# Layer 0 of a hybrid decoder trunk: the second value group and the second gate group multiplied as one pair, with seven products for eight on half of the rows

## The chip, the core and the metric

The kernel runs on one core of one Trainium2 chip. The core has TensorE (PE, matrix multiply; its weight loads are shown as PEld), VectorE (DVE), ScalarE (ACT), GpSimd (POOL) and SyncE (SP). Here POOL and SP do little else than start transfers from HBM. Each engine works through its own queue in a fixed order; engines wait for each other through semaphores. The metric is the device time of one execution in microseconds (us); the program is built once with a fixed order on every engine.

## What is computed

The input is 256 tokens of 2048 numbers in float32. Layer 0 norms them and multiplies by one wide weight, `w_in` (2048 x 6144). Its columns feed an RG-LRU (x and y, eight blocks of 128 columns each) and eight HGRN2 heads (query q and forget gate f, 128 columns a head, a value v and an output gate g):

```python
proj = h @ w_in
x_lru, y_lru, q_h, f_h, v_h, g_h = jnp.split(proj, list(IN_SPLITS), axis=-1)
lru = rg_lru(causal_depthwise_conv(x_lru, conv_w, conv_b), w_a, b_a, w_i, b_i, lam)
lru = lru * jax.nn.gelu(y_lru.astype(F32), approximate=True)
hg = hgrn2(q_h, f_h, v_h, g_h, lower_bound, g_norm)
mixed = jnp.concatenate([lru, hg], axis=-1).astype(h.dtype)
return mixed @ w_out
```

An output projection with residual, a squared-ReLU MLP, an attention layer (layer 1) and a second MLP follow. The change concerns v and g of heads 4 to 7 only: 512 columns of v and 512 of g, each of them 256 tokens x 2048 rows of weight.

## The kernel before

**Arithmetic.** Every float32 factor is split into a high part (rounded to the fast matmul format, fp32r) and a low remainder. A product takes three matmuls: high x high, high x low, low x high. For a weight tile, class `Weights` does the split: a copy on ACT makes `hi` (line 109), a subtraction on DVE makes `lo` (line 110). A *unit* is one weight tile of 128 partitions x 2048 columns (1 MB). It goes through pools of three buffers each: `raw` from HBM, `hi`, `lo`.

**Plan of units.** `units` lists all weight tiles in the order of use. `fetch()` starts a unit's load on SP's queue and issues its split, some three units ahead of use, with raised priority (`stream`). `unit()` hands the split tile to its user. The mixer of layer 0 is written as a string of steps (`ORDER`): `v0`, `v1` value groups and `k0`, `k1` gate groups (four units each), `h0` to `h7` heads (two units each), `x0` to `x7` and `y0` to `y7` LRU blocks (one unit each), `g0`, `g1` LRU gates (one unit each). A scheduler then fixes each engine's order by priorities: work that is not urgent is put where an engine would be free by its estimate. The matmuls `mm` stay in the written order.

**Value and gate groups.** `tokens()` multiplies a group: two PSUM banks (one for each half of the 256 tokens), four units, each unit with 4 blocks of 128 rows. That is 2 x 16 x 3 = 96 matmuls with 512 columns. The transposed, scaled input lies in `bufa` as 16 blocks of 128 rows, high and low. ACT takes the result out of PSUM with the factor `rt`, one over the root mean square of each token; the gate group then gets `v * sigmoid(v)` (lines 428 to 430).

**The first norm.** `rt` comes from `xtok`, the input by tokens, which lies in `xall` (its view by tokens is called `xres`) and stays there as the residual until the output projection adds to it (line 598). ACT squares it (line 272), DVE forms the mean and its inverse square root in 13 small steps (lines 276 to 305), PE turns the result over tokens (line 288). Because this is needed soon, the second half of the low part of units 6 and 7 (the third and fourth unit of `k0`) must come after the last step of the root on DVE:

```python
behind[6] = behind[7] = [roots[-1]]
```

**Seven products.** The later layers already multiply with `blocks()`. It takes two column groups of weights together, and on the first 8 of 16 row blocks it forms seven products for eight: the four quarters of the input (two halves of tokens, even and odd row blocks) and the four quarters of the weights are combined by sums beforehand, in the manner of Strassen and Winograd. The sums over the input are called *forms* (in the output projection lines 634 and 584 to 587, then a cast, 580, and a subtraction, 581). The sums over the weights are made on DVE (lines 141 and 161) and by accumulating loads on POOL's queue (lines 153 and 163), in two arrays `t1` and `s` of 1 MB each. The order of a pair is a, t1, t2, n, c, n, t3, d, n, t4, n: seven products and four plain units of the other 8 row blocks (each with two products). One product is 4 blocks x 3 = 12 matmuls of 512 columns.

**Heads.** After q and f, a head runs a chain: a multiplication on DVE (line 484) and a small matmul on PE (line 467) alternate seven times, then come line 462 and lines 491 to 493. The chains are spread between the large matmuls of later steps.

Of the kernel before, what the change touches and what calls it, by code (L numbers as in the profile page):

```python
# [20 lines left out]
P = 128  # L21
S = 256
# [20 lines left out]
def trunk_kernel(ctx, tc, begin, xtok, cols, tab, masks, pos, fin, w_in, w_gate, w_out, w_qkv, w_o, w1, w2, out):  # L43
# [31 lines left out]
    def order(src, i):  # L75
        return LASTS if src is w2 and i == 120 else ORDERS
# [21 lines left out]
    class Weights:  # L98
# [17 lines left out]
        def part(self, at, n):  # L116
            return self.hi[:, at:at + n], self.lo[:, at:at + n]
# [17 lines left out]
    def combine(u, src, i, what, i0):  # L135
        def load(name, j, home=wraw):
            held[name] = home.tile([P, 2048], F32, name="raw" if home is wraw else name)
            nc.sync.dma_start(held[name], src[j])

        def add(to, x, y):  # L140
            V.tensor_tensor(held[to], held[x], held[y], OP.add)
# [12 lines left out]
        if ahead == ("t4",) and src is w2 and i0 != BOUNDARY:  # L154
            add("s", "s", "d")
        w = made[u] = Weights(held[{"t1": "s", "t2": "s", "t3": "t1", "t4": "s"}.get(what, what)],
                              1024 if what == "t2" else 2048, follow=what == "t2" or u and units[u - 1][2:3] == ("t2",))
        if what == "t1":
            for at in (0, 1024):
                s = held["s"][:, at:at + 1024]  # L160
                V.tensor_tensor(s, s, held["c"][:, at:at + 1024], OP.add)  # L161
        if what == "c" and (src is not w2 or i0 == BOUNDARY):
            nc.gpsimd.dma_start(held["s"], src[i0 + 1], accum_op=OP.add)
# [28 lines left out]
    def mm(*args, **kw):  # L192
        chain[:] = [after(T.matmul(*args, **kw), chain)]  # L193
# [7 lines left out]
    def put_off(wait, *fs):  # L201
        later.extend((clock[0] + wait, f) for f in fs)
# [215 lines left out]
    def hgrn_v(i):  # L418
# [3 lines left out]
                A.activation(v[:, j], v[:, j], AF.Copy, scale=rt[:, j:j + 1])  # L422
        return v

    def hgrn_g(i):
        v = tokens_group(w_in, 16 + i * 16, rt, name="gg")
        for j in range(2):
            z = wk.tile([P, 512], F32, name="gs", bufs=1)
            lut(z, v[:, j], AF.Sigmoid)
            V.tensor_tensor(v[:, j], v[:, j], z, OP.mult)  # L430
        return v

    def hgrn(hd, vg, gg):
# [112 lines left out]
    def lru_out(b):  # L546
# [8 lines left out]
        V.tensor_tensor(y, y, xc[:, b], OP.mult)  # L555
        split_to(bufb[:, b], y)

    vgroups, ggroups = {}, {}
    for step in ORDER.split():
        i = int(step[1])  # L560
        if step[0] == "v":
# [16 lines left out]
    def part_forms(f, k, m, at, src):  # L578
        hi, lo = (f[:, k:k + m, h].rearrange("p m (f c) -> p m f c", f=4)[:, :, at] for h in range(2))
        A.copy(hi, src)  # L580
        V.tensor_tensor(lo, src, hi.bitcast(F32), OP.subtract)

    def combos(s1, s2, s3, s4, a11, a21, a12, a22):
        V.tensor_tensor(s1, a21, a22, OP.subtract)
        V.tensor_tensor(s3, a11, a21, OP.subtract)
        V.tensor_tensor(s2, s1, a11, OP.subtract)
        V.tensor_tensor(s4, a12, s2, OP.add)
# [40 lines left out]
    def out_project(src, gname, off):  # L628
        nrm = Norm()

        def forms(k):
            z = pair.tile([P, 2, 2, P], F32, name="y21", bufs=2)
            h, l = (bufb[:, k + off:k + off + 2, c * S:c * S + S].bitcast(F32) for c in range(2))
            V.tensor_tensor(z.rearrange("p i j c -> p i (j c)"), h, l, OP.add)
            a11, a21, a12, a22 = (z[:, i, j] for i in range(2) for j in range(2))
            combos(a22, a11, a21, a12, a11, a21, a12, a22)
            part_forms(formh, k // 2, 1, slice(0, 4), z.rearrange("p i j (one c) -> p one (i j) c", one=1))

        put_off(4, *(lambda k=k: forms(k) for k in range(0, 8, 2)))
# [6 lines left out]
    cosT = cst.tile([P, 2, 16], F32, name="cosT")  # L646
    sinT = cst.tile([P, 2, 2, 16], F32, name="sinT")


    def blocks(src, i0, n0, mov, forms, events, final, off=0):  # L650
        part = lambda k, c: mov[:, (k + off) % KB, c * P:c * P + P]
        plain = lambda j, k: (part(k, j), part(k, 2 + j))
        form = lambda f, k: (forms[:, k, 0, f * P:f * P + P], forms[:, k, 1, f * P:f * P + P])
        side = {"a": lambda i: plain(0, 2 * i), "d": lambda i: plain(0, 2 * i + 1), "t4": lambda i: plain(1, 2 * i + 1),
                "t1": lambda i: form(3, i), "t2": lambda i: form(0, i), "t3": lambda i: form(1, i),
                "c": lambda i: form(2, i)}
        alpha, delta, gamma = (pmm.tile([P, 512], F32, name="p") for _ in range(3))
        beta = psc.tile([P, 512], F32, name="pt" if src is w_qkv else "po" if n0 else "pd", bufs=1)
        bank = {"a": beta, "t1": alpha, "t2": beta, "c": alpha, "t3": beta, "d": gamma, "t4": beta}
        sums = {(0, 0): gamma, (0, 1): beta, (1, 0): alpha, (1, 1): delta}  # L660
        opened = [gamma, delta]
        starts = {"a": (gamma, beta), "t1": (delta, alpha)}

        def times(bank, w, get):
            for i in range(4):
                h, l = w.part(i * 512, 512)
                xh, xl = get(i)
                mm(bank, xh, h, start=not any(b is bank for b in opened), stop=False, skip_group_check=True)
                opened.append(bank)
                mm(bank, xh, l, start=False, stop=False, skip_group_check=True)  # L670
                mm(bank, xl, h, start=False, stop=i == 3, skip_group_check=True)

        plains, twice = [0, 0, 0, 0], {}
        for what, u, *js in order(src, i0 + 4 * n0):
            if js != [(1,)]:
                w = unit(src, None if u is None else i0 + 4 * n0 + u)
                twice[u] = w
            else:
                w = twice[u]
            if what != "n":  # L680
                times(bank[what], w, side[what])
                if what in starts:
                    with urgent():
                        A.copy(*starts[what])
                if what in events:
                    events[what](bank[what])
                flush(1, 1)
                continue
            n, g = divmod(u, 4)
            for j in js[0] if js else (1, 0) if n or src is w_qkv else (0, 1):  # L690
                times(sums[n, j], w, lambda i, j=j, g=g: plain(j, 4 * g + i))
                plains[2 * n + j] += 1
                if plains[2 * n + j] == 2:
                    final(n, j, sums[n, j])
                flush(1, 1)

    def to_h(n, tiles):
        def work():
# [370 lines left out]
def _layout(a):  # L1069
# [14 lines left out]
    wi = n(a["rec_w_in"][0])  # L1084
    fx = feat(wi[:, :2048])
    fq = feat(wi[:, 2048:4096])
    fg = toks(wi[:, 5120:])
    fv = toks(wi[:, 4096:5120])
    w_in = [fx]
    for g in range(2):  # L1090
        if g:
# [50 lines left out]
```

## Time and profile before

| | |
|---|---|
| median of 3 runs | 2135.94 us (2135.84 to 2135.94) |
| the profiled execution | 2135.02 us |
| its span, first to last instruction | 2133.1 us |
| PE busy | 2122.7 us |
| DVE busy | 1776.4 us |
| ACT busy | 1372.5 us |
| POOL busy | 65.0 us |
| mean granted clock of TensorE | 0.999 |

The profile is of one execution. Times inside it count from the span's start. The page gives the busy time of each engine; the chain goes back from the last instruction through what released each step; the timeline lists instructions in order (start, duration, engine, line, operation; out<-in with shapes; xN means N merged instructions; in brackets the engine's idle time ahead of it and what ended it); the table of windows gives each engine's busy time in a stretch. Matmuls overlap, so the duration of one is longer than its distance to the next. An fp32 matmul that is not split (the small ones of the heads) shows as two records. A few per cent of the matmul records can be missing.

### The profile page before, as it was taken

The page shows a single profiled execution, that of the slowest core. Times are in us where ns is not written, and L with a number is a line of the kernel's source. Part 1 is how long each engine was busy: PE and PEld are TensorE (multiplying, and loading weights), DVE is VectorE, ACT ScalarE, POOL GpSimd, SP SyncE. Part 2 cuts the span into 40 slices and gives each one's busy share as a digit, 9 for nine tenths or more (in the row PEclk, how much of TensorE's full clock was granted, in tenths as well). Part 3 has the DMA queues.
Part 4 walks back from the last instruction along what each step waited for, and adds up shares of the span by engine and source line. Part 5 has one row for each costly group of instructions (what it writes and reads, how often), then busy time and mean ns, then how long its engine had stood idle before and what let it go on. Part 6 is the DMA issues. An engine that isn't in the chain of part 4 may idle for free.

```text
span 2133.1 us, 26744 instructions
## 1 busy us (share of the span) xinstructions
PE 2122.7 (100%) x10554; PEld 1799.9 (84%) x10554; DVE 1776.4 (83%) x1961; ACT 1372.5 (64%) x1545; POOL 65.0 (3%) x83
## 2 busy tenths in 40 slices
PE   9999999999999999999999999999999999999998
PEld 8989998888888888888888888888888888888886
DVE  7767888888888888888987777698887888888887
ACT  7445565766576567567667767666756765755764
POOL 0000000000000000000000000000000000000000
PEclk9999999999999999999999999999999999999999
DMA  8444446686777677777887667667767768777873
GB/s 340 158 173 157 160 145 217 212 271 227 236 239 254 221 238 253 236 242 232 265 272 224 230 208 250 233 217 226 248 234 252 238 209 266 243 234 226 272 225 145
DMA packets 69518, 486.62 MB, mean 228 GB/s; under 512 B 7776, under 2 KB 8288, under 8 KB 11920
## 3 DMA queue, kind: packets, MB, share of 16 engines
q1 hardware_dynamic: 58176, 410.96, 51.2%
q0 software_dynamic: 10928, 73.60, 17.8%
q8 instruction: 83, 1.36, 0.3%
q10 hardware_dynamic: 288, 0.34, 0.0%
q14 instruction: 43, 0.35, 0.0%
HBM read 480.68 MB, written 4.19 MB: 227 GB/s over the span
## 4 chain that ended last, share of the span: by engine, by line
PE 98%; ACT 1%; DVE 1%; DMA 0%; issue 0%; ACTq 0%; DVEq 0%
PE p L193 62%; PE po L193 14%; PE pd L193 12%; PE pt L193 5%; PE pl L196 2%; PE pl L467 1%; PE pl L193 0%; ACT hi L109 0%; DMA raw<-in_w 0%; DVE lo L110 0%; PE po L252 0%; PE pd L196 0%; PE pd L451 0%; PE pl L462 0%; PE po L492 0%
## 5 line engine op out<-in xcount | busy, mean ns | idle before, releaser
L110 DVE TENSOR_TENSOR lo<-raw,hi 128x2048 fp32r<-128x2048 f32 (+2 forms) x406 | 790.1, 1955 | 174.6 <-ACT hi L109 169.8
L109 ACT CAST hi<-raw 128x2048 fp32r<-128x2048 f32 (+2 forms) x406 | 660.1, 1643 | 338.4 <-PE p L193 178.8
L193 PE MATMUL p<-hi,bufa 128*128 128x512 f32 x1488 | 481.6, 394 | 0.0
L193 PE MATMUL p<-hi,bufb 128*128 128x512 f32 x1264 | 406.6, 391 | 0.0
L193 PEld LDWEIGHTS p<-hi,bufa 128*128 128x128 f32 x1488 | 279.4, 188 | 56.6
L110 DVE TENSOR_TENSOR lo<-s,hi 128x2048 fp32r<-128x2048 f32 (+1 forms) x160 | 279.0, 1754 | 27.4 <-ACT hi L109 26.3
L109 ACT CAST hi<-s 128x2048 fp32r<-128x2048 f32 (+1 forms) x160 | 236.7, 1480 | 98.9 <-DVE s L161 54.7
L193 PE MATMUL p<-lo,bufa 128*128 128x512 f32 x744 | 287.5, 390 | 0.0
L193 PEld LDWEIGHTS p<-hi,bufb 128*128 128x128 f32 x1264 | 237.2, 188 | 48.9
L193 PE MATMUL p<-lo,bufb 128*128 128x512 f32 x632 | 246.0, 389 | 0.0
L193 PE MATMUL p<-bufa,hi 128*128 128x256 f32 x1024 | 193.2, 287 | 0.0
L193 PEld LDWEIGHTS p<-lo,bufa 128*128 128x128 f32 x744 | 139.9, 188 | 27.4
L193 PEld LDWEIGHTS p<-bufa,hi 128*128 128x128 f32 x1024 | 161.2, 191 | 0.2
L193 PE MATMUL p<-bufa,lo 128*128 128x256 f32 x512 | 146.5, 286 | 0.0
L109 ACT CAST hi<-t 128x2048 fp32r<-128x2048 f32 x40 | 76.6, 1914 | 99.9 <-PE p L193 91.4
L110 DVE TENSOR_TENSOR lo<-t,hi 128x2048 fp32r<-128x2048 f32 x40 | 91.7, 2292 | 57.7 <-ACT hi L109 57.3
L193 PEld LDWEIGHTS p<-lo,bufb 128*128 128x128 f32 x632 | 118.7, 188 | 24.0
L193 PE MATMUL p<-hi,formx 128*128 128x512 f32 x352 | 115.8, 390 | 0.0
L193 PE MATMUL po<-hi,bufb 128*128 128x512 f32 x320 | 103.5, 390 | 0.0
L193 PEld LDWEIGHTS p<-bufa,lo 128*128 128x128 f32 x512 | 98.1, 192 | 0.0
L193 PE MATMUL p<-hi,formh 128*128 128x512 f32 x288 | 94.5, 389 | 0.0
L161 DVE TENSOR_TENSOR s<-s,raw 128x1024 f32<-128x1024 f32 x80 | 94.0, 1216 | 0.0
(301 smaller groups left out, 3208.2 us busy)
## 6 DMA issues: line engine op xcount, KB each, us to landing
raw<-in_w SPq DMA_DIRECT2D x224, 1024.0 KB, 6.0
raw<-in_w_in SPq DMA_DIRECT2D x44, 1024.0 KB, 4.8
raw<-in_w_qkv SPq DMA_DIRECT2D x42, 1024.0 KB, 6.9
t<-in_w SPq DMA_DIRECT2D x32, 1024.0 KB, 4.9
t<-in_w POOLq DMA_DIRECT2D x32, 1024.0 KB, 8.6
s<-in_w POOLq DMA_DIRECT2D x17, 1024.0 KB, 8.5
raw<-in_w_out SPq DMA_DIRECT2D x15, 1024.0 KB, 4.9
raw<-in_w_o SPq DMA_DIRECT2D x15, 1024.0 KB, 4.9
```

What stands on the lines that cost most here:

```text
L109: a = A.copy(h, w)
L110: v = V.tensor_tensor(l, w, h.bitcast(F32), OP.subtract)
L161: V.tensor_tensor(s, s, held["c"][:, at:at + 1024], OP.add)
L193: chain[:] = [after(T.matmul(*args, **kw), chain)]
L196: chain[:] = [after(T.transpose(out_, in_, ident), chain)]
L467: T.matmul(pl[:, j], kq[:, js], halves(qp[:, js], c, True), start=True, stop=True)
```

## The change

`v1` and `k1` become one step `p1`, which runs `blocks()` on `w_in` from unit 28 on. Four new steps `f0` to `f3` make the forms of the input's first 8 row blocks. The forms lie in parts of `bufb` that are still free then (blocks 12 to 15 and 4 to 7). The weight sums `t1` and `s` use the two halves of `xall`, which after the first norm holds only the residual; after the pair, `xtok` is loaded a second time through POOL's queue. `blocks()` gets a case for `w_in`: three PSUM banks at first, and the fourth when it comes to `d`; some partial results are taken out of PSUM by ACT and completed by additions on DVE (`put`, `add`). The weights of the second groups are laid out in the order of `PAIRED`. The step string also has x3, h3 and x0 behind the pair instead of ahead of the groups, some other LRU blocks in another order, and y7 ahead of y3. `part_forms`, `combos` and `blocks` are moved up in the file; `forms` of the output projection becomes `pair_forms`.

```diff
     for step in ORDER.split():
+        if step[0] == "p":
+            plan2(w_in, 28)
+        if step[0] not in where:
+            continue
...
         if what == "a":
-            load("t1", i0 + 4, both)
+            if src is w_in:
+                held["t1"], held["s"] = xall[:, :2048], xall[:, 2048:]
+                nc.sync.dma_start(held["t1"], src[i0 + 4])
+            else:
+                load("t1", i0 + 4, both)
+                held["s"] = both.tile([P, 2048], F32, name="s")
             load("a", i)
-            held["s"] = both.tile([P, 2048], F32, name="s")
             add("s", "a", "t1")
...
         alpha, delta, gamma = (pmm.tile([P, 512], F32, name="p") for _ in range(3))
-        beta = psc.tile([P, 512], F32, name="pt" if src is w_qkv else "po" if n0 else "pd", bufs=1)
+        if src is w_in:
+            beta, gamma = gamma, None
+        else:
+            beta = psc.tile([P, 512], F32, name="pt" if src is w_qkv else "po" if n0 else "pd", bufs=1)
...
-        opened = [gamma, delta]
-        starts = {"a": (gamma, beta), "t1": (delta, alpha)}
+        opened, starts = [], {}
+        if src is not w_in:
+            opened, starts = [gamma, delta], {"a": (gamma, beta), "t1": (delta, alpha)}
...
+            if what == "d" and bank["d"] is None:
+                bank["d"] = sums[0, 0] = pmm.tile([P, 512], F32, name="p")
...
+    def pair_forms(forms, k, src, z):
+        h, l = (src[:, k:k + 2, c * S:c * S + S].bitcast(F32) for c in range(2))
+        V.tensor_tensor(z.rearrange("p i j c -> p i (j c)"), h, l, OP.add)
+        a11, a21, a12, a22 = (z[:, i, j] for i in range(2) for j in range(2))
+        combos(a22, a11, a21, a12, a11, a21, a12, a22)
+        part_forms(forms, k % 8 // 2, 1, slice(0, 4), z.rearrange("p i j (one c) -> p one (i j) c", one=1))
...
+    def values_gates():
+        both_ = [vgs.tile([P, 2, 512], F32, name=n) for n in ("vg", "gg")]
+        rn = tmp.tile([P, 2], F32, name="rn0", bufs=1)
+        V.tensor_scalar(rn, rt, -1.0, None, op0=OP.mult)
+
+        def put(n, j, r=rt):
+            def event(bank):
+                with urgent():
+                    A.activation(both_[n][:, j], bank, AF.Copy, scale=r[:, j:j + 1])
+            return event
+
+        def add(n, j, bank, r=rt):
+            o = both_[n][:, j]
+            with urgent():
+                V.scalar_tensor_tensor(o, bank, r[:, j:j + 1], o, op0=OP.mult, op1=OP.add)
+
+        def final(n, j, bank):
+            if (n, j) == (0, 1):
+                put(n, j)(bank)
+            else:
+                add(n, j, bank)
+            if (n, j) == (1, 0):
+                gated(both_[1], 0)
+
+        def u3(bank):
+            add(1, 1, bank, rn)
+            gated(both_[1], 1)
+
+        blocks(w_in, 28, 0, bufa, form0,
+               {"a": put(0, 0), "t1": put(1, 1), "t2": put(1, 0, rn), "t3": u3}, final)
+        for j in range(2):
+            nc.gpsimd.dma_start(xres[:, j], xtok[:, j])
+        return both_
...
+        if step[0] == "f":
+            pair_forms(form0, 2 * i, bufa, wk.tile([P, 2, 2, P], F32, name="fz", bufs=1))
+        elif step[0] == "p":
+            vgroups[1], ggroups[1] = values_gates()
...
-ORDER = "v0 k0 h0 h1 h2 x1 x3 h3 x0 k1 v1 x2 h4 x4 g0 x5 h5 h6 x6 y0 y1 h7 x7 g1 y3 y7 y4 y2 y5 y6"
+ORDER = "v0 k0 h0 f0 f1 h1 f2 f3 x1 h2 p1 h3 x3 x2 h4 x0 x5 g0 x4 h5 h6 x6 y0 y1 h7 x7 g1 y7 y3 y4 y2 y5 y6"
```

More of the change, by code (lines that the diff above doesn't have):

```diff
@@ L423, in hgrn_v, with gated @@
         return v
+    def gated(v, j):
+        z = wk.tile([P, 512], F32, name="gs", bufs=1)
+        lut(z, v[:, j], AF.Sigmoid)
+        V.tensor_tensor(v[:, j], v[:, j], z, OP.mult)
     def hgrn_g(i):
@@ L556, in lru_out, with part_forms, combos @@
         split_to(bufb[:, b], y)
+    def part_forms(f, k, m, at, src):
+        hi, lo = (f[:, k:k + m, h].rearrange("p m (f c) -> p m f c", f=4)[:, :, at] for h in range(2))
+        A.copy(hi, src)
+        V.tensor_tensor(lo, src, hi.bitcast(F32), OP.subtract)
+    def combos(s1, s2, s3, s4, a11, a21, a12, a22):
+        V.tensor_tensor(s1, a21, a22, OP.subtract)
+        V.tensor_tensor(s3, a11, a21, OP.subtract)
+        V.tensor_tensor(s2, s1, a11, OP.subtract)
+        V.tensor_tensor(s4, a12, s2, OP.add)
@@ new lines, in blocks, with times @@
+    def blocks(src, i0, n0, mov, forms, events, final, off=0):
+        part = lambda k, c: mov[:, (k + off) % KB, c * P:c * P + P]
+        plain = lambda j, k: (part(k, j), part(k, 2 + j))
+        form = lambda f, k: (forms[:, k, 0, f * P:f * P + P], forms[:, k, 1, f * P:f * P + P])
+        side = {"a": lambda i: plain(0, 2 * i), "d": lambda i: plain(0, 2 * i + 1), "t4": lambda i: plain(1, 2 * i + 1),
+                "t1": lambda i: form(3, i), "t2": lambda i: form(0, i), "t3": lambda i: form(1, i),
+                "c": lambda i: form(2, i)}
+        alpha, delta, gamma = (pmm.tile([P, 512], F32, name="p") for _ in range(3))
+        if src is w_in:
+            beta, gamma = gamma, None
+        else:
+            beta = psc.tile([P, 512], F32, name="pt" if src is w_qkv else "po" if n0 else "pd", bufs=1)
+        bank = {"a": beta, "t1": alpha, "t2": beta, "c": alpha, "t3": beta, "d": gamma, "t4": beta}
+        sums = {(0, 0): gamma, (0, 1): beta, (1, 0): alpha, (1, 1): delta}
+        opened, starts = [], {}
+        if src is not w_in:
+            opened, starts = [gamma, delta], {"a": (gamma, beta), "t1": (delta, alpha)}
+        def times(bank, w, get):
+            for i in range(4):
+                h, l = w.part(i * 512, 512)
+                xh, xl = get(i)
+                mm(bank, xh, h, start=not any(b is bank for b in opened), stop=False, skip_group_check=True)
+                opened.append(bank)
+                mm(bank, xh, l, start=False, stop=False, skip_group_check=True)
+                mm(bank, xl, h, start=False, stop=i == 3, skip_group_check=True)
+        plains, twice = [0, 0, 0, 0], {}
+        for what, u, *js in order(src, i0 + 4 * n0):
+            if js != [(1,)]:
+                w = unit(src, None if u is None else i0 + 4 * n0 + u)
+                twice[u] = w
+            else:
+                w = twice[u]
+            if what == "d" and bank["d"] is None:
+                bank["d"] = sums[0, 0] = pmm.tile([P, 512], F32, name="p")
+            if what != "n":
+                times(bank[what], w, side[what])
+                if what in starts:
+                    with urgent():
+                        A.copy(*starts[what])
+                if what in events:
+                    events[what](bank[what])
+                flush(1, 1)
+                continue
+            n, g = divmod(u, 4)
+            for j in js[0] if js else (1, 0) if n or src is w_qkv else (0, 1):
+                times(sums[n, j], w, lambda i, j=j, g=g: plain(j, 4 * g + i))
+                plains[2 * n + j] += 1
+                if plains[2 * n + j] == 2:
+                    final(n, j, sums[n, j])
+                flush(1, 1)
@@ new lines, in pair_forms, with __getitem__ @@
+    def pair_forms(forms, k, src, z):
[4 more added lines that the diff above has]
+        part_forms(forms, k % 8 // 2, 1, slice(0, 4), z.rearrange("p i j (one c) -> p one (i j) c", one=1))
+    class Apart:
+        def __getitem__(self, at):
+            k = at[1]
+            i = k.start if isinstance(k, slice) else k
+            b = bufb[:, (12, 4)[i // 2]:][:, :4].rearrange("p (k h) c -> p k h c", h=2)
+            return b[(at[0], slice(i % 2, i % 2 + 1) if isinstance(k, slice) else i % 2) + at[2:]]
@@ new lines, in trunk_kernel @@
+    form0 = Apart()
+    def values_gates():
[9 more added lines that the diff above has]
+            o = both_[n][:, j]
+            with urgent():
+                V.scalar_tensor_tensor(o, bank, r[:, j:j + 1], o, op0=OP.mult, op1=OP.add)
+        def final(n, j, bank):
+            if (n, j) == (0, 1):
+                put(n, j)(bank)
+            else:
+                add(n, j, bank)
[9 more added lines that the diff above has]
+        return both_
@@ L576, in open_pairs @@
         return pool_, pool_.tile([P, 4, 2, 512], F32R, name="formh")
[L578 to L587, printed above, removed]
     both = ctx.enter_context(tc.tile_pool(name="both", bufs=1))
@@ L629, in out_project @@
         nrm = Norm()
[L631 to L639, printed above, removed]
+        put_off(4, *(lambda k=k: pair_forms(formh, k + off, bufb, pair.tile([P, 2, 2, P], F32, name="y21", bufs=2))
+                     for k in range(0, 8, 2)))
         for n in range(2):
@@ L647, in trunk_kernel @@
     sinT = cst.tile([P, 2, 2, 16], F32, name="sinT")
[L650 to L657, printed above, removed]
-        beta = psc.tile([P, 512], F32, name="pt" if src is w_qkv else "po" if n0 else "pd", bufs=1)
-        bank = {"a": beta, "t1": alpha, "t2": beta, "c": alpha, "t3": beta, "d": gamma, "t4": beta}
-        sums = {(0, 0): gamma, (0, 1): beta, (1, 0): alpha, (1, 1): delta}
-        opened = [gamma, delta]
-        starts = {"a": (gamma, beta), "t1": (delta, alpha)}
[L664 to L695, printed above, removed]
@@ L1086, in _layout @@
     fq = feat(wi[:, 2048:4096])
-    fg = toks(wi[:, 5120:])
-    fv = toks(wi[:, 4096:5120])
+    fg, fv = (np.concatenate([toks(w[:, :512]), toks(w[:, 512:], PAIRED)]) for w in (wi[:, 5120:], wi[:, 4096:5120]))
     w_in = [fx]
```

6 lines of the change are left out of this document (2 added, 4 removed).

## The prediction, made before the changed kernel had run

> **What bounds the kernel now.** I read the page first, then the table of windows over the first layer's mixer, then the chain of work that ended last.
>
> ```profile
> PE 2122.7 (100%) x10554; PEld 1799.9 (84%) x10554; DVE 1776.4 (83%) x1961; ACT 1372.5 (64%) x1545; POOL 65.0 (3%) x83
> PE 98%; ACT 1%; DVE 1%; DMA 0%; issue 0%; ACTq 0%; DVEq 0%
> ...
> core 0: us, PE busy (x) PEld busy (x) DVE busy (x) ACT busy (x) POOL busy (x), PEclk, DMA share, GB/s
> 0.00:40.00 40.00, 38.95 (x172) 33.17 (x173) 31.57 (x106) 32.46 (x64) 0.89 (x5) 1.00 0.88 348
> 40.00:80.00 40.00, 40.00 (x297) 38.18 (x297) 26.15 (x43) 19.86 (x26) 0.00 (x0) 1.00 0.62 213
> 120.00:160.00 40.00, 40.00 (x204) 33.88 (x203) 25.48 (x55) 18.09 (x28) 0.00 (x0) 1.00 0.51 177
> 200.00:240.00 40.00, 40.00 (x341) 40.00 (x341) 35.45 (x95) 28.76 (x59) 0.00 (x0) 1.00 0.46 156
> 280.00:320.00 40.00, 39.73 (x328) 38.96 (x327) 35.24 (x89) 30.62 (x63) 0.00 (x0) 1.00 0.42 146
> ```
>
> TensorE is the bound: 98% of the chain is PE, and in the mixer it stands still for 1.05 us at the start and 0.27 us near 285 us. So a matmul taken away is worth its full time, and any wait put before a matmul costs its full time. There is hardly a stall that the change could remove. The margin lies in VectorE: 25 us of 40 where the second groups stand now (120:160), 35 of 40 after them.
>
> **Matmuls.** The two groups are 2 x 2 x 16 x 3 = 192 matmuls of 512 columns. Afterwards 7 x 4 x 3 = 84 do the first eight rows of blocks and 96 the rest: 180. The order of the changed program's matmul queue has 12 fewer and is otherwise made of the same shapes. The chain has one product of twelve by itself:
>
> ```profile
> 6.55 34.36 PE p L193 x151
> 415.77 2.72 PE pd L193 x12
> ```
>
> Term one: -2.72 us, all on the path.
>
> **Forms (f0 to f3), new.** Four times a sum over 512 columns, four combinations of 128, a cast on ACT and a subtraction over 512. The same lines run today in the output projection:
>
> ```profile
> 342.91 1.29 DVE L581 TENSOR_TENSOR formh<-y,formh 128x512 fp32r<-128x512 f32 x2
> 344.11 1.29 DVE L634 TENSOR_TENSOR y<-bufb 128x512 f32<-128x512 f32 x2
> 345.31 0.49 DVE L584 TENSOR_TENSOR y<-y 128x128 f32<-128x128 f32 x2
> 345.71 0.29 DVE L585 TENSOR_TENSOR y<-y 128x128 f32<-128x128 f32 x1
> L580 ACT CAST formh<-y x40: 606/620/632, 341.4 to 2023.8; 128x512 fp32r<-128x512 f32 x40
> ```
>
> Two of 512 start 1.20 us before what follows, two of 128 0.40 us: a form is 0.6 + 4 x 0.2 + 0.6 = 2.0 us of VectorE, the four 8.0, and 4 x 0.62 = 2.5 us of ACT. In the order of the changed program they do not lie after h0 where the step string puts them, but as filling in the opening and in the first gate group. There they meet this:
>
> ```profile
> 23.51 3.08 DVE L110 TENSOR_TENSOR lo<-raw,hi 128x512 fp32r<-128x512 f32 x3
> 27.82 0.62 PE L193 MATMUL p<-lo,bufa 128*128 128x512 f32 x2
> 31.28 0.17 DVE L871 TENSOR_SCALAR sinT<-ang 128x32 f32<-128x32 f32 x1
> 33.51 0.62 ACT L272 ACTIVATE z<-xall 128x512 bf16<-128x512 f32 x1
> 34.26 0.16 DVE L276 TENSOR_REDUCE nm<-ss 128x2 f32<-128x8 f32 x1 [2.80 <-ACT z L272]
> 35.56 1.22 DVE L110 TENSOR_TENSOR lo<-raw,hi 128x1024 fp32r<-128x1024 f32 x1
> 37.68 0.16 DVE L305 SCALAR_TENSOR_TENSOR nr<-rs,nr 128x2 f32<-128x2 f32 x1
> 37.76 3.49 DVE L110 TENSOR_TENSOR lo<-raw,hi 128x1024 fp32r<-128x1024 f32 x3
> 40.74 0.38 PE L288 MATMUL pt<-tab__199,nr 128*128 128x128 f32 x2
> 40.88 0.48 PE L193 MATMUL p<-lo,bufa 128*128 128x512 f32 x1
> ```
>
> These rows are the root of the first norm: ACT squares (L272), 13 small VectorE steps from L276 to L305, then the second half of the third gate unit's low part (its first half is the row at 35.56), which `behind` orders after the root. At 40.74 PE turns the root and at 40.88 needs that second half. It begins at 37.76, takes 1.14 and is ready 2.0 us early. I add up what the changed order puts ahead of it:
> - Start of the root. VectorE was free at 31.45 and waited 2.80 us for ACT. Ahead of L276 now stand all of f0 and f1 and f2 short of its last combination and its subtraction: 2.0 + 2.0 + 1.2 = 5.2 us, of which some 0.6 falls into small gaps of the opening. VectorE arrives at 31.45 + 4.6 = 36.0. ACT, with one cast among the squares and the first group ending 0.3 late (f0 makes the third and fifth low blocks of the opening just too late), would have been ready at 35.2. So the root starts at 36.0, 1.8 late.
> - Length of the root. It was 37.76 - 34.26 = 3.50 us. Now the last combination of f2 (0.2), its subtraction (0.6), the sum of f3 (0.6), three of its combinations (0.6) and the first half of the fourth unit's low part (1.14) lie in it, 3.1 us, of which 0.6 fills latency between dependent steps: about 6.0 us.
> - So the second half begins at 42.0 and is ready at 43.2, against 40.9 needed. Term two: +2.3 us, on the path. Behind that wait on PE stands everything. Next late would be the fourth unit's halves, which follow at 1.14 each and are needed 5 us later: covered.
>
> Bounds of term two: 0 if the order's filling falls into idle time on the chip as well (2.80 us were idle), 4.0 if none of it does (5.2 + 3.1 against the margins of 2.8 and 2.0, and 0.5 for the opening). I take 2.3, nearer to the upper end, because the filling is in the queue ahead of the waiting rows and not beside them.
>
> **The pair itself.** Eleven units are prepared instead of eight, and weights are added up.
>
> ```profile
> 350.42 0.69 DVE L598 SCALAR_TENSOR_TENSOR xall<-p,xall 128x512 f32<-128x512 f32 x1 [0.39 <-PE p L193]
> 353.97 2.28 DVE L141 TENSOR_TENSOR s<-raw,t 128x2048 f32<-128x2048 f32 x1
> 364.14 2.29 DVE L110 TENSOR_TENSOR lo<-raw,hi 128x2048 fp32r<-128x2048 f32 x1 [1.32 <-ACT hi L109]
> L161 DVE TENSOR_TENSOR s<-s,raw 128x1024 f32<-128x1024 f32 x80 | 94.0, 1216 | 0.0
> raw<-in_w_in SPq DMA_DIRECT2D x44, 1024.0 KB, 4.8
> s<-in_w POOLq DMA_DIRECT2D x17, 1024.0 KB, 8.5
> ```
>
> VectorE: 3 more low parts x 2.2, one sum 2.2, two half sums x 1.14, four additions from PSUM x 0.6 = 13.5 us more. ACT: three more casts of about 1.9 = 5.7 us; its four copies from PSUM stay four. Between the first product and the next head, 43 us of PE, the changed VectorE queue holds 36 us including the tails of h0 to h2, so it is covered. Walking the queue with these rows, each low part of the pair is ready 1 to 5 us before its product; the tightest is the first whole unit, 0.9 us. The sum of the first two units waits in VectorE's queue for two loads; the later of them can start when x1's low part is made, 10 us before the sum; h2's low part behind it has 5 us. On SP's queue the load into the residual's array needs no slot, so nothing stands behind it. On POOL two accumulating loads, 8.5 us each, come 30 and 10 us before their use; the two reloads of the residual stand behind them and before the next accumulate, some 200 us before the residual is read. DMA has room: share 0.51 in 120:160, and two accumulates and two reloads are new. Price: 0.
>
> **The order of steps.** x3, h3 and x0 move from before the groups to behind them. From the end of the pair to the eighth y the queues hold 113 us of VectorE beside 132 of PE. On average covered, but around the first gates the margins between a chain's multiplication and its matmul shrink from this
>
> ```profile
> 221.12 0.42 DVE L484 TENSOR_TENSOR qk<-qk,tot 128x256 f32<-128x256 f32 x1
> 222.60 0.55 PE L467 MATMUL pl<-qk 128*128 128x64 f32 x4
> ```
>
> (1.1 us) to 0.3 to 0.5 us by the same walk, at four places. Bounds: 0 if the walk is right, about 1 us at each of the four if VectorE is 1.4 us later. I take +0.5, nearer zero, as a late chain lets the next work slide in. y3 and y7 trade places at no cost: same shapes, same queues from h6 on.
>
> **Sum.** -2.72 + 2.3 + 0.5 = +0.1. The profiled execution took 2135.02, its span 2133.1; the median of the runs is 2135.94, 0.9 above it. I apply the sum to the median: 2136.0 us. 0.2% is 4.3 us, about what a measurement can tell from no change.
>
> **Rivals.**
> - The saving arrives whole: the forms run in VectorE's idle time before the root. For it: the 2.80 us idle above. Against it: their place ahead of the low half. 2135.9 - 2.7 = 2133.2. To pass -4.3 us another 1.6 would have to come from stalls of which the mixer shows 0.3.
> - Slower: the dense stretch after the pair. At 35 of 40 us VectorE has 5 us in 40; were each operation there waiting 0.15 us more on ACT or PE, the 180 rows between pair and h6 would lose 27 us against 19 of slack, so it decides once VectorE falls 19 us behind: then PE waits 27 - 19 = 8 us, less the 2.7 saved: 2141.
> - TensorE's clock falls in the wait at the root. Cold and warm price of one shape:
>
> ```profile
> 1.05 5.49 PE po L252 x24
> 67.10 0.45 PE pd L451 x4
> ```
>
> 229 ns against 112. If a wait of 2.3 to 4 us starts another such 5.5 us, half of it is lost: 2136.0 + 2.7 = 2138.7. Against it: the clock is 1.00 in every window. The Trainium skill, "TensorE: Matmul & The Clock Gate", section "Part 1: The HAM clock gate", says that an idle window of about 3.4 us brings the clock back to half, and as much activity releases it; by that rule a wait of 2.3 us would mostly escape and one of 4 us would not. No row of this trace has an idle time to test it.
>
> **How the numbers follow.** Forecast 0.63; saving whole 0.17; dense stretch 0.13; clock 0.07. All but the dense case and part of the clock case lie within 0.2%: faster 0.04, same 0.79, slower 0.17. The range goes from the whole saving with the mixer's small stalls (2132.6) to the dense case (2141.5). Within the forecast's own case: 2134 to 2138.
>
> **What the profile after would show.** 12 matmuls of 512 columns fewer. PE waiting 2 to 3 us near 41 us for L114 or the root. No PE wait inside the pair. VectorE near 36 of 40 us from 130 to 170. PE's end of the mixer within 1 us of today's. I am wrong if PE shows no wait near 41 us, or waits of several us after the pair.

## The result and the profile after

The changed kernel takes 2165.14 us, median of four runs (2164.73 to 2165.76), against 2135.94 us: 1.0139 times as long, 95% interval 1.0127 to 1.0150. That is 29.2 us slower, and 23.6 us beyond the upper end of the predicted range.

The page of the changed kernel, its busy times and its chain, and then the table of windows over the first layer's mixer (columns as in the prediction):

```profile
PE 2151.1 (99%) x10542; PEld 1797.9 (83%) x10542; DVE 1798.5 (83%) x1989; ACT 1380.8 (64%) x1545; POOL 67.6 (3%) x87
PE 97%; DVE 1%; ACT 0%; DMA 0%; issue 0%; SPq 0%; ACTq 0%; DVEq 0%
...
0.00:40.00 40.00, 38.25 (x165) 31.60 (x166) 33.56 (x116) 31.69 (x65) 0.89 (x5) 1.00 0.95 372
40.00:80.00 40.00, 38.21 (x271) 35.57 (x270) 30.17 (x51) 21.80 (x28) 0.86 (x1) 1.00 0.55 192
120.00:160.00 40.00, 40.00 (x251) 35.94 (x250) 31.02 (x60) 19.70 (x27) 0.55 (x1) 1.00 0.65 234
200.00:240.00 40.00, 40.00 (x341) 40.00 (x340) 35.70 (x93) 28.98 (x58) 0.00 (x0) 1.00 0.43 146
280.00:320.00 40.00, 39.71 (x328) 38.93 (x328) 35.02 (x91) 29.61 (x62) 0.00 (x0) 1.00 0.43 151
```

From here on a *product* is one matmul of 512 columns. TensorE has 12 products fewer and is busy 28.4 us longer. In the first 80 us it is idle for 2.5 us more than before; from there on no wait of it is longer than 0.4 us. The loss is busy time. To see where, the same three places are looked up in the timelines of TensorE: the last products ahead of the root's transposition, the first matmul of 256 columns behind the first gate group, and the first product behind the mixer. Before:

```profile
40.29 0.61 PE L193 MATMUL p<-hi,bufa 128*128 128x512 f32 x2
...
50.27 0.40 PE L193 MATMUL p<-bufa,hi 128*128 128x256 f32 x2
...
328.17 0.40 PE L193 MATMUL p<-hi,bufb 128*128 128x512 f32 x1
```

After:

```profile
41.93 0.61 PE L201 MATMUL p<-hi,bufa 128*128 128x512 f32 x2
43.63 0.43 PE L296 MATMUL pt<-tab__199,nr 128*128 128x128 f32 x2 [1.09 <-DVE nr L313]
44.77 0.50 PE L201 MATMUL p<-lo,bufa 128*128 128x512 f32 x1 [0.70 <-DVE lo L114]
...
54.19 0.40 PE L201 MATMUL p<-bufa,hi 128*128 128x256 f32 x2
...
329.16 0.40 PE L201 MATMUL p<-hi,bufb 128*128 128x512 f32 x1
```

Ahead of the root's transposition the changed kernel is 1.64 us late, behind the first gate group 3.92, and when the mixer ends 0.99. The whole part that the diff rewrites costs 1 us. The other 29.9 us of the 30.9 us between the spans (2164.0 and 2133.1) arise behind it, where both programs issue the same instructions in the same order. There the chain shows it. Before, and then after, three groups of twelve products each, not the same three (start, us, what):

```profile
1911.33 2.72 PE p L193 x12
1914.05 2.72 PE pd L193 x12
1916.77 2.72 PE po L193 x12
```

```profile
1903.31 2.80 PE p L201 x12
1906.11 2.80 PE pd L201 x12
1908.91 2.80 PE p L201 x12
```

Twelve products take 2.80 us instead of 2.72: 233 ns from start to start instead of 227, at a granted clock of 1.00. The table of groups by shape tells which products these are (line, engine, operation, out<-moving,stationary, count, busy us, mean ns of one). Before, then after:

```profile
L193 PE MATMUL p<-hi,bufa 128*128 128x512 f32 x1488 | 481.6, 394 | 0.0
L193 PE MATMUL p<-hi,bufb 128*128 128x512 f32 x1264 | 406.6, 391 | 0.0
L193 PE MATMUL p<-hi,formx 128*128 128x512 f32 x352 | 115.8, 390 | 0.0
```

```profile
L201 PE MATMUL p<-hi,bufa 128*128 128x512 f32 x1448 | 469.6, 395 | 0.7 <-ACT hi L113 0.7
L201 PE MATMUL p<-hi,bufb 128*128 128x512 f32 x1296 | 425.2, 397 | 0.0
L201 PE MATMUL p<-hi,formx 128*128 128x512 f32 x352 | 117.9, 396 | 0.0
```

Products whose stationary operand (the second name) is bufa are as fast as before; those with bufb or formx take 6 ns more each, and so do those with formh. A product's duration in this table includes its tail, which overlaps the next, so the difference counts and not the 397.

What do bufb, formx and formh have in common? They lie behind the pool tmp in each partition, whereas bufa, the raw weights and their halves hi and lo lie ahead of it. The change adds one small tile to tmp: `rn = tmp.tile([P, 2], F32, name="rn0", bufs=1)`, 8 bytes that take a slot of 32. The start addresses in the two programs are, in bytes:

```
                 before     after     after modulo 64
bufa              23328     23328     32
hi, first buffer  80672     80672     32
lo, first buffer 105248    105248     32
bufb             132384    132416      0
formx            165152    165184      0
formh            197920    197952      0
```

4728 products of 512 columns read their stationary operand from the three arrays that moved. At 6.4 ns that is 30.3 us. This is the theory (A) that the experiments test; the rival (B) is that the changed work leaves something behind it (order, DMAs, the shifted wk).

### The profile page after: what moved, and what is told of

It is laid out like the page before. It is cut to its first block, busy times and chain, and to the rows that moved or that the text cites. A ratio compares the mean times of both kernels' runs of the same rounds, so it can differ in the third digit from the quotient of the medians.

```text
span 2164.0 us, 26759 instructions
## 1 busy us (share of the span) xinstructions
PE 2151.1 (99%) x10542; PEld 1797.9 (83%) x10542; DVE 1798.5 (83%) x1989; ACT 1380.8 (64%) x1545; POOL 67.6 (3%) x87
## 4 chain that ended last, share of the span: by engine, by line
PE 97%; DVE 1%; ACT 0%; DMA 0%; issue 0%; SPq 0%; ACTq 0%; DVEq 0%
PE p L201 61%; PE po L201 14%; PE pd L201 13%; PE pt L201 4%; PE pl L204 2%; PE pl L478 1%; DVE lo L114 1%; PE pl L201 0%; DMA first<-in_begin 0%; ACT hi L113 0%; PE pd L204 0%; DVE bufa L250 0%; PE pd L462 0%; ACT bufa L249 0%; PE pl L473 0%
## 5 line engine op out<-in xcount | busy, mean ns | idle before, releaser
L201 PE MATMUL p<-hi,bufa 128*128 128x512 f32 x1448 | 469.6, 395 | 0.7 <-ACT hi L113 0.7
L201 PE MATMUL p<-hi,bufb 128*128 128x512 f32 x1296 | 425.2, 397 | 0.0
L201 PEld LDWEIGHTS p<-hi,bufa 128*128 128x128 f32 x1448 | 272.1, 188 | 57.2 <-ACT hi L113 1.1
L201 PEld LDWEIGHTS p<-hi,bufb 128*128 128x128 f32 x1296 | 243.4, 188 | 57.7
L201 PE MATMUL p<-lo,bufa 128*128 128x512 f32 x724 | 280.2, 391 | 0.7 <-DVE lo L114 0.7
L201 PE MATMUL p<-lo,bufb 128*128 128x512 f32 x648 | 256.2, 395 | 0.0
L201 PEld LDWEIGHTS p<-lo,bufa 128*128 128x128 f32 x724 | 136.0, 188 | 28.4 <-DVE lo L114 1.5
```

## The experiments

**The new tile made 64 bytes wide (changed kernel).**

```
-        rn = tmp.tile([P, 2], F32, name="rn0", bufs=1)
+        rn = tmp.tile([P, 16], F32, name="rn0", bufs=1)[:, :2]
```

> The changed kernel with its new small tile rn0 64 bytes wide instead of 8 (it then takes 64 bytes of a partition and not 32), so that bufb, formx and formh, which lie behind it, start at 32 modulo 64 as before the change (132448) and not at 0 (132416). Nothing else differs. Theory A: a product of 512 columns takes 6.5 ns longer where its stationary operand starts at another place modulo 64 than before; 4728 products read theirs from those three arrays, 4728 x 6.5 ns = 30.7 us, so 2165.1 - 30.7 = 2134.4 us, with 227 ns from start to start in every such row; the PE waits of 1.1 and 0.7 us near 43 us stay. Rival B: the loss comes from the changed order of work, the forms or the additional DMAs; then 2165 us, with 233 ns as in the changed kernel.

Measured: 2166.2 us, 1.0142 times the kernel before (1.0125 to 1.0159). By the numbers on record this is B: nothing came back. But it leaves two readings. Either the addresses don't matter, or a shift of 64 is as bad as one of 32. The next run decides between the two.

**The kernel before, with a shift of 32 bytes and no other edit.**

```
-        r2n = tmp.tile([P, 2], F32, name="r2n", bufs=1)
+        r2n = tmp.tile([P, 16], F32, name="r2n", bufs=1)[:, :2]
```

> The kernel before with its tile r2n 64 bytes wide instead of 8 (two steps of 32 bytes instead of one), so that bufb, formx and formh move by 32 bytes, from 32 to 0 modulo 64, and every instruction stays as it was. Theory A: 4680 products x 6.5 ns = +30.4 us, 2166.4 us. Rival B: 2136 us.

Measured: 2164.7 us, 1.0135 (1.0115 to 1.0156). Its groups by shape:

```profile
L193 PE MATMUL p<-hi,bufa 128*128 128x512 f32 x1488 | 482.1, 394 | 0.3 <-ACT hi L109 0.3
L193 PE MATMUL p<-hi,bufb 128*128 128x512 f32 x1264 | 414.2, 397 | 0.0
L193 PE MATMUL p<-hi,formx 128*128 128x512 f32 x352 | 117.9, 396 | 0.0
```

Not one instruction of the change is in this kernel, and it is as slow as the changed one, in the same groups. Rival B is out: the address alone costs 28.8 us. What of the address counts was still to be found.

**All arrays shifted by 32, and the weights alone shifted by 32 (kernel before).** Both make one tile wider: the first in front of everything, the second between bufa and the raw weights, and r2n once more, so that bufb and the forms' arrays come to lie at 32 modulo 64 again.

```
-    spare = cst.tile([P, 1], F32, name="spare")
+    spare = cst.tile([P, 16], F32, name="spare")[:, :1]
```
```
-    bufa = act.tile([P, KB, 2 * S], F32R, name="bufa")
+    bufa = act.tile([P, KB * 2 * S + 8], F32R, name="bufa")[:, :KB * 2 * S].rearrange("p (k c) -> p k c", k=KB)
```

> The kernel before with 32 bytes more in front of all arrays: bufa, the weights' halves hi and lo, bufb, formx and formh all start at 0 modulo 64. Theory A1 (a stationary operand at a multiple of 64 is slow by itself): all 7968 products of 512 columns lose 6.5 ns, +51.8 us, 2188 us. Theory A2 (what counts is that the stationary operand and the moving weights lie alike modulo 64): 2136 us. Rival B: 2136 us.

> The kernel before with the weights' arrays (raw, hi, lo) alone moved to 0 modulo 64; bufa, bufb, formx and formh stay at 32. Theory A1: the stationary operands lie as before, 2136 us, but for the products of 256 columns, whose stationary operand is hi or lo: 1632 x 6.5 ns = up to +10.6, 2147 us. Theory A2: every product has operands that lie unlike, 7968 x 6.5 = +51.8 us, 2188 us and up to 2198. Rival B: 2136 us.

Measured: 2135.75 us with all shifted (1.000, 0.999 to 1.001), 2179.75 us with the weights alone (1.0206, 1.0185 to 1.0226). So no array's own place matters. What matters is how the activations lie to the weights (A2). In the second kernel all 7968 products of 512 columns are slow (mean 233 to 236 ns from start to start, against 227 to 231 before). It stays 8 us below the expected 2188. Set against the kernel before row by row, the products lost 6.0 ns on average and not 6.5, and the matmuls of 256 columns, in which the weights are stationary, became 1 to 2 ns faster; that is about 6 of the 8 us, the rest is open.

**Many distances in one kernel.** hi's buffers 128 bytes further apart, lo's 96.

```
-            self.hi = whi.tile([P, 2048], F32R, name="hi")
-            self.lo = wlo.tile([P, 2048], F32R, name="lo")
+            self.hi = whi.tile([P, 2080], F32R, name="hi")[:, :2048]
+            self.lo = wlo.tile([P, 2072], F32R, name="lo")[:, :2048]
```

> The kernel before with the weight buffers spread: hi's three buffers 128 bytes further apart, lo's three 96, so that the distance from a product's stationary operand to its moving weights takes six values modulo 512 against bufa (0, 128, 256; 384, 480, 64) and six against bufb, formx and formh (352, 480, 96; 224, 320, 416); before, all are 0 modulo 512. To make room the attention keeps 7 transposed tiles instead of 8. Read by buffer. Theory A2 with modulus 512: about 227 ns from start to start at distance 0 alone, 233 at all others; then some 8/9 of 7968 products lose 6.5 ns, about +46 us, 2182 us. Modulus 256: also 227 at 256. Modulus 128: also 227 at 128, 256 and 384. An open alternative is that some distance is faster than 227.

Measured: 2175.9 us (one run). From start to start, by the distance from the stationary operand to the moving weights, behind the opening, without gaps over 300 ns:

```
distance modulo 512, bytes    0     64    96    128   224   256   320   352   384   416   480
mean ns                     232.1 232.0 233.8 231.7 231.8 231.9 234.6 233.8 230.8 230.6 231.0
```

No distance is faster than the 227 of the kernel before, and here even distance 0 is slow. hi and lo, which follow one another in the stream of products, lay unlike each other too, so that the run could not give the modulus. The next two take the two questions apart.

**Distance 128 and 256, hi and lo alike; and lo alone apart (kernel before).** The first widens bufa by 128 bytes and r2n by 256; the second puts a gap of 32 bytes in front of lo, and widens r2n until bufb lies like hi again.

```
+    pool("gap").tile([P, 8], F32, name="gap")
     wlo = pool("wlo", 3)
```

> The kernel before with 128 bytes more between bufa and the weights and 256 more between the weights and bufb: a product's moving weights lie at 128 modulo 512 from bufa, and at 256 from bufb, formx and formh; hi and lo stay alike. If likeness counts modulo 128, both kinds stay at 227 ns and the time is 2136 us. If modulo 256, the 3288 products with bufa lose 6.4 ns each, +21 us, 2157 us, and those with bufb stay at 227. If modulo 512, all lose, as where the weights were moved by 32: 2180 us.

> The kernel before with lo's buffers alone moved by 32 bytes; hi, bufa, bufb, formx and formh stay alike modulo 512. Of three products in a row two stream hi and one lo. If a product is slow where its own stationary and moving operand lie unlike, the 2656 products that stream lo lose 6.4 ns, +17 us, 2153 us, and those that stream hi stay at 227. If neighbours in the stream must lie alike too (what the mixed kernel with all distances suggests, where even distance 0 took 232 ns), all lose: 2180 us.

Measured: 2153.1 us (1.0080, 1.0061 to 1.0099) and 2176.5 us (1.0189, 1.0170 to 1.0209). The groups of the first:

```profile
L193 PE MATMUL p<-hi,bufa 128*128 128x512 f32 x1488 | 488.9, 399 | 1.5 <-ACT hi L109 1.2 <-DVE bufa L242 0.3
L193 PE MATMUL p<-hi,bufb 128*128 128x512 f32 x1264 | 406.5, 391 | 0.0
L193 PE MATMUL p<-hi,formx 128*128 128x512 f32 x352 | 116.6, 392 | 0.0
```

At 256 from the weights bufb is as fast as before (391), at 128 bufa is slow (399 against 394). Of the distances tried with hi and lo alike, 0 and 256 are fast and 32, 64 and 128 slow, so what counts is likeness modulo 256. The products with formx, at 256 too, lost some 1.5 ns (392 against 390 in the tables); why is open. The groups of the second (its lines are one further down):

```profile
L194 PE MATMUL p<-hi,bufb 128*128 128x512 f32 x1264 | 412.1, 395 | 0.0
L194 PE MATMUL p<-lo,bufa 128*128 128x512 f32 x744 | 294.3, 399 | 0.2 <-DVE lo L111 0.2
L194 PE MATMUL p<-lo,bufb 128*128 128x512 f32 x632 | 252.3, 399 | 0.0
```

Products that stream hi, whose own two operands lie alike, went from 391 to 395 as well. It is not enough that a product's own operands lie alike; the weights of its neighbours have to lie alike too.

**The change without its shift.** rn0 comes from wk, which lies behind the three arrays.

```
-        rn = tmp.tile([P, 2], F32, name="rn0", bufs=1)
+        rn = wk.tile([P, 2], F32, name="rn0", bufs=1)
```

> The changed kernel with rn0 taken from the pool wk behind bufb instead of tmp in front of it: bufb, formx and formh keep the addresses that they had before the change (132384, 165152, 197920), and every instruction and its order is that of the changed kernel. This is the change without its shift of addresses. In the changed kernel's trace the first layer's mixer ends 1.05 us later than before, of which 48 products of the pair with bufb account for 0.3, so theory A expects 2135.95 + 0.8 = 2136.8 us; the predicted sum was +0.1, 2136.0. Rival B (an interplay with the shifted wk, or the order of work) would leave it above 2160.

Measured: 2136.65 us against 2135.76, ratio 1.0003 (0.9994 to 1.0012), no difference that can be told. Theory A expected 2136.8 and rival B above 2160. This is the change that the prediction priced. Its timeline at the root, and its windows there:

```profile
43.12 0.43 PE L296 MATMUL pt<-tab__199,nr 128*128 128x128 f32 x2 [1.10 <-DVE nr L313]
44.26 0.50 PE L201 MATMUL p<-lo,bufa 128*128 128x512 f32 x1 [0.70 <-DVE lo L114]
44.60 1.00 PE L201 MATMUL p<-hi,bufa 128*128 128x512 f32 x2
45.39 0.63 PE L201 MATMUL p<-lo,bufa 128*128 128x512 f32 x1
...
48.24 0.63 PE L201 MATMUL p<-hi,bufa 128*128 128x512 f32 x2
```

```profile
40.00:45.00 5.00, 3.19 (x14) 2.12 (x14) 5.00 (x13) 3.98 (x6) 0.00 (x0) 0.97 0.02 8
45.00:50.00 5.00, 5.00 (x17) 3.97 (x16) 3.48 (x6) 0.62 (x1) 0.00 (x0) 0.69 0.95 334
```

The two waits are those of the changed kernel. Behind them the granted clock falls (0.69 in 45 to 50), two products take 1.00 us instead of 0.63, and 3.4 us later it is back. In the changed kernel's own profile the same waits of 1.09 and 0.70 us left the clock at 1.00. Followed product by product the two kernels differ there by 1.6 us, the price of the rival "clock". The times of the eleven executions suggest that this fall comes in some of them only: six have a mean granted clock of 0.998 and took 2136.65 to 2137.5 us (median 2137.0), five have 0.999 and took 2134.02 to 2135.66 us (median 2135.3). Only one of the eleven has a trace, so the split is inferred; its 1.7 us are half of the 3.4 us at half clock.

**The forms later.** As the run before, with the forms' steps ahead of h0 and each form's first sum ordered behind the low half prepared last (`line[1:]`); then the same with the steps x3, h3, x0 and y3 in the old order.

```
-ORDER = "v0 k0 h0 f0 f1 h1 f2 f3 x1 h2 p1 h3 x3 x2 ..."
+ORDER = "v0 k0 f0 f1 f2 f3 h0 h1 x1 h2 p1 h3 x3 x2 ..."
...
-        V.tensor_tensor(z.rearrange("p i j c -> p i (j c)"), h, l, OP.add)
+        after(V.tensor_tensor(z.rearrange("p i j c -> p i (j c)"), h, l, OP.add), wait)
```

> As the run before, and the four forms are kept out of the opening: their steps stand between k0 and h0, and the first sum of each form has to follow the low half of the weights prepared last, which is the first of h0's units. The changed kernel's 3.9 us by the end of the first gate group (1.1 + 0.7 of PE waits near 43 us, about 2 us of opening groups that end later) should go, if they come from the forms ahead of the root: 2136.8 - 3.9 = 2132.9 us, 3 us below the kernel before, with no PE wait near 41 us. If the forms are not the cause, 2136.8. If the forms come too late for the pair's first form product, PE waits between 105 and 125 us and the time lies in between.

> As the run with the forms later, with the steps in the order of the kernel before: the pair stands where k1 and v1 stood, x3, h3 and x0 ahead of it, and y3 ahead of y7. The run with the forms later gave back 3.9 us between 200 and 206 us. If that came from the heads and gates moved behind the pair (the rival of the dense stretch), the saving now arrives: 2135.8 - 2.7 = 2133.1 us, PE without a wait from 160 to 260 us. If the pair then lacks cover, since more heads' work stands ahead of it beside the forms, PE waits between 110 and 170 us and the time is 2136 or more.

Measured: 2135.94 us (1.0000, 0.9991 to 1.0009), and 2143.6 us (1.0037, 1.0023 to 1.0051). Both expected about 2133. The waits near 43 us are gone in both, and both run 2.1 to 2.5 us ahead of the kernel before from the pair to some 195 us and 230 us. Then the dense stretch takes it back. The first, in its waits up to 260 us and its windows:

```profile
PE pl L478 <- DVE qk L495: 0.6, 1, 0.6
PE p L201 <- ACT bufb L246: 0.5, 1, 0.5
PE po L502 <- ACT st L488: 0.4, 1, 0.4
```

```profile
195.00:200.00 5.00, 3.49 (x21) 2.78 (x21) 5.00 (x11) 3.57 (x8) 0.00 (x0) 0.93 0.46 138
200.00:205.00 5.00, 5.00 (x34) 5.00 (x33) 2.83 (x9) 2.49 (x7) 0.00 (x0) 0.73 0.45 187
```

And the second:

```profile
280.00:285.00 5.00, 3.19 (x23) 2.56 (x21) 5.00 (x16) 2.60 (x8) 0.00 (x0) 1.00 0.45 133
285.00:290.00 5.00, 4.86 (x21) 4.57 (x22) 1.91 (x6) 1.40 (x4) 0.00 (x0) 0.51 0.20 80
340.00:345.00 5.00, 2.06 (x5) 1.43 (x6) 5.00 (x14) 0.91 (x3) 0.00 (x0) 0.81 0.91 334
```

In each, VectorE is busy 5.00 of 5.00 us, PE waits 1.5 to 2.9 of them, and then the clock falls. These are the predicted rivals "dense stretch" and "clock", at other places and in kernels whose queues came out in another order than the changed kernel's. The second run shows that the old order of steps is no cure: its queues differ in the tail as well.

**Three forms behind the root, the rest untouched.** The same edits, but only f1, f2 and f3 wait, and for the last step of the root (`roots[-1:] if i else ()`). From the pair on, the queues of TensorE and VectorE then are those of the changed kernel.

> The changed kernel with bufb's addresses as before the change, the forms' steps between k0 and h0, and f1, f2 and f3 (not f0) ordered behind the last step of the first norm's root. The order of steps is the changed kernel's, and from the pair on VectorE's and TensorE's queues are those of the changed kernel, so that the dense stretch, which cost that kernel nothing, stays as it is. If the root's waits are the whole price of the change besides the addresses, PE waits less than 0.3 us near 41 us, no half clock follows, and the saving arrives: 2135.8 - 2.7 + 0.3 for f0 in the opening = 2133.4 us, within 0.6. If removing the wait only brings the next one (VectorE then has less lead after the pair, as in the run with the forms later), the time is 2135 to 2137 us with waits between 190 and 240 us.

Measured: 2133.12 us (2132.49 to 2133.94) against 2135.70, ratio 0.9988 (0.9979 to 0.9997). This one is 2.6 us faster than the kernel before. Waits of 1.2 and 0.4 us stand in its opening, none near 41 us. Its first matmul of 256 columns behind the first gate group and its first product behind the mixer:

```profile
52.21 0.40 PE L201 MATMUL p<-bufa,hi 128*128 128x256 f32 x2
...
327.37 0.40 PE L201 MATMUL p<-hi,bufb 128*128 128x512 f32 x1
```

It is 1.94 us behind the kernel before at the first of these rows, all of it from the opening, and 0.80 ahead at the second: 2.74 us, the 12 products.

## Why the prediction was wrong, step by step

- **Matmuls, -2.72: right.** From the pair's first product to its last the kernel with the old addresses gained 2.8 us on the kernel before, and the changed kernel 2.6, since 48 of its products there have bufb as stationary operand and took some 4 ns more.
- **Forms, +2.3 on the path: right in place, and in size at the root; the opening was priced too low.** PE waited 1.09 us for the root and 0.70 for the low half behind it; the lag grew from 1.64 to 3.92 us there, so 2.3. But 2.3 was to be the whole lag behind the first gate group, with the opening's first group taken as 0.3 late; the whole lag was 3.92. The rows of VectorE's timeline in the changed kernel show the mechanism:

```profile
37.40 0.15 DVE L284 TENSOR_REDUCE nm<-ss 128x2 f32<-128x8 f32 x1
43.42 0.15 DVE L313 SCALAR_TENSOR_TENSOR nr<-rs,nr 128x2 f32<-128x2 f32 x1
43.49 2.35 DVE L114 TENSOR_TENSOR lo<-raw,hi 128x1024 fp32r<-128x1024 f32 x2
```

  From the root's first step to the low half behind it 6.1 us passed where 6.0 were worked out; it began at 37.4 instead of 36.0, as VectorE came to it later. How much of the opening's 1.64 us is the forms' is open: in three traces with the changed opening the lag was 0.8 to 1.6 us, and in two of kernels with the unchanged instructions (32 bytes more ahead of bufb, or ahead of everything) 0.4 and 0.9.
- **The pair, 0: right.** No wait of PE from 60 to 280 us above 0.2 us. VectorE was busy 31 of 40 us in 120:160 and from 130 to 170, below the 36 of 40 named as a sign; its load was overrated.
- **The order of steps, +0.5: 0.8 too high.** In the rest of the mixer the lag shrank, from 1.3 to 1.0 us.
- **The sum, +0.1: near for the instructions** (2136.0 predicted, 2136.65 with rn0 out of the way), **and wrong for the kernel.** That it came so near is partly luck: the opening cost more than taken and the order of steps less, and the 2136.65 lies between executions at 2135.3 and at 2137.0. The failing step is the one where the sum is applied to the whole time. It took for granted that all work behind the mixer keeps its duration because its instructions and their order are the same. The change's list of parts has no entry for rn0's slot in tmp, and none for the arrays that it pushes by 32 bytes. Their price was 30 us, eleven times the gain.
- **The rivals.** None of them had this mechanism, so the range could not hold the result. "The saving arrives whole" is what the kernel with three forms behind the root does. "The dense stretch", smaller than its 8 us of waiting, and "the clock" were seen in other runs: the clock at 1.6 us against the 2.7 taken, behind less idle time than thought (below).
- **The signs named beforehand.** Twelve matmuls fewer, waits of 2 us near 41, none inside the pair, the mixer's end within 1 us: all as said. VectorE's 36 of 40 us did not come. None of these signs could show the 30 us, which were lost in a place that the prediction had not looked at.

## What to carry to other kernels

A new tile is also a shift: compare the addresses of the large arrays before and after, not only the instructions, and put small tiles into the pool that lies last. In this kernel the products ran at 227 ns only where stationary operands and weights start alike modulo 256 bytes, and lost some 6 ns each at the other distances tried; a time that changes in groups of instructions which the diff doesn't touch points to such a cause, and padding the old kernel by the same amount tests it. Filling that a scheduler pulls ahead of a short serial chain costs what exceeds the chain's slack where the chain feeds TensorE, here 2.3 us for some 8 us of filling; with three of the forms behind the chain's last step the change gains 2.6 us, while moving all of them changed the queues further down and gave that away.

## What the runs showed of the hardware that was not expected

- **Where the operands start.** Stationary operand and weights alike modulo 256 bytes: 227 ns per product of 512 columns; 32, 64 or 128 apart: 232 to 234 ns; hi and lo 32 apart from each other, 231 (hi) to 236 ns (lo), though hi and the stationary operand lie alike. Matmuls of 256 columns with stationary weights went the other way by 1 to 2 ns. Why is open. The Trainium skill, "SBUF — State Buffer", section "Who interferes with whom", gives TensorE two independent read ports, one for the moving operand and one for the weight load, and lets only the port pair of VectorE and GpSimd cause contention. The runs here show that the time of a product depends on how these two operands lie to each other (227 against 233 ns), which two independent reads would not lead one to expect; whether the reads meet at a port, or what else it is, no run here shows.
- **The clock falls after less than a whole idle window.** Two waits of 1.10 and 0.70 us within 2.3 us were followed by 3.4 us at half clock in the kernel with rn0 moved, and not in the changed kernel, which had the same waits. The Trainium skill, "TensorE: Matmul & The Clock Gate", section "Part 1: The HAM clock gate", says that a window of about 3.4 us runs freely, and that an idle one halves the clock. The length of 3.4 us agrees with these runs, and windows that run freely agree with a fall in one execution and none in another; that the window must be idle throughout does not, as PE was idle for 1.8 us of the 3.4 ahead of the fall and worked in the rest.
